# Two-layer decoder trunk on one core: gates of the first three expert groups kept on chip, first chunk's dots two steps later, scatter adds regrouped

## The chip, the core and the metric

The kernel runs on one core of a Trainium2 chip. A core has TensorE (PE: matmuls, with weight loads beside them), VectorE (DVE), ScalarE (ACT), GpSimd (POOL) and SyncE (SP); each runs its own queue of instructions in order, and they wait for each other by semaphores. SP, ACT and POOL also issue DMA transfers. The metric is the device time of one execution in microseconds (us), the median of several runs; less is better.

## The reference

512 tokens of width 1024 pass through two layers. Layer 0 mixes tokens with causal mean pooling and retention, layer 1 with a gated linear recurrence. After each mixer stands a PEER channel mixer, and after each of the four a layer norm. The change touches PEER alone:

```python
q = (xt @ w_q).reshape(T, PEER_HEADS, 2, PEER_HALF)
s = jnp.einsum('thpd,hpkd->thpk', q, sub_keys)
s_top, i_top = lax.top_k(s, PEER_TOPK)
...
best, pos = lax.top_k(cand, PEER_TOPK)
eid = jnp.take_along_axis(cand_id, pos, axis=-1)
gate = jax.nn.softmax(best, axis=-1)
...
act = jax.nn.gelu(jnp.einsum('td,thkd->thk', xt, u_sel), approximate=False)
coef = gate * act
return jnp.einsum('thk,thkd->td', coef, v_sel)
```

Each token has 8 heads. A head scores two sets of 128 sub-keys, takes the 16 best of each, and of their 256 sums the 16 best again: 16 of 16384 experts with a softmax gate. An expert is a row `u` and a row `v`; the output is the sum of gate x gelu(x.u) x v over the 128 chosen experts of a token.

## The kernel before

**Dense and gathered tokens.** For tokens 64 to 383 the kernel computes x.u for all 16384 experts, multiplies by a gate matrix that is zero where an expert wasn't chosen, and multiplies the product by all of `v`. For the last 128 tokens it fetches the chosen rows of `u` and `v` one by one. For the first 64 tokens it fetches the chosen `u` rows while it routes, and takes their `v` part in the dense product. Every fp32 operand of a matmul is split into a high and a low part (`split`, lines 172 to 174: `hi` on ACT, `lo` on VectorE), and each product is three matmuls (lines 189 to 191 in `mm3`, line 1142 in `mm2`).

**Groups and tiles.** Experts come in 128 blocks of 128, four blocks to a group (`NB`), so 32 groups (`NG`). `mm1` streams a block of `peer_ut`, multiplies and puts gelu(x.u) into `ge`. The gates of a group are a tile `gt` of 12 slices of 32 tokens by 4 blocks: slices 0 to 3 (the first 128 tokens) come from the DRAM array `gz`, slices 4 to 11 from the DRAM array `gd`.

**Routing** (`route_topk`). The query projection comes in four chunks of two heads. For each chunk, `steps` takes the 16 best for the token blocks 0, 1, 2, 3 (`top16`, four yields each), and `choose` picks the experts of the first block right after its own step. `Scatter.place` then fetches 16 rows of `u` per chunk on POOL (`urow`, line 745; two token halves share a row tile, and eight tiles go round), `Scatter.dots` multiplies them on VectorE (line 109), spread over later steps by the table `DOTS[chunk][token block][step]`. `Scatter.weigh` multiplies gelu into the gates (lines 115 and 117), and `Scatter.add` scatters gates into `gz` by accumulating indirect DMAs on POOL (line 131), 32 per chunk, 128 per layer, in portions after the table `ADDS`. Adds of one head don't wait for each other; the first of a head waits for those of the head before to have landed. Adds are queued behind the last row fetch (`issue_after(self.fetch)`).

**Dense gates** (`route_gates`). For each of eight slices VectorE builds one-hot matrices (`oh`, `og`, lines 924 and 925), TensorE multiplies them, ACT scales the result into the slice buffer `gbuf` (two buffers, line 936), and SP writes it to `gd` for all 32 groups (line 940).

**Lookahead.** While this runs, `lookahead` computes `mm1` for the first 25 groups (`NLA`). A generator yields costs, and for each 2.8 of credit one block of lookahead is issued: `Y2`, `YA` and `YB` are such costs. Groups 23 and 24 stay on chip (`KEEP`); the others are written to the DRAM array `sp` and read back. What is left is issued behind the routing.

**Experts** (`experts`). The groups come in a fixed order that begins with 28, 23, 24: group 28's blocks aren't looked ahead, so its `mm1` comes at the start of this stage, on TensorE in front of the first `mm2`. `fetch` reads a group's `ge` and `gt`: for the first two groups `gd` on SP and `gz` on POOL, for the others on ACT. `Scatter.read` (line 142) waits for all adds of the last head. `high` multiplies gates and `ge` on VectorE (line 1087) and casts the high part `ch` on ACT (line 1091), `low` makes `cl` on VectorE (line 1098), and `mm2` multiplies `ch`, `cl` by the two parts of `v` (line 1142). Between these, `gather_rounds` fetches the rows for the last 128 tokens on POOL (line 992) with dots (line 1004) and sums (line 1017) on VectorE.

The code is traced in the order in which it stands; a scheduler then places the instructions into the engines' queues by their dependences and priorities, so a queue's order may differ from the code's. Pools of tiles are opened and closed like a stack: the memory of a closed pool is used again, and the new user waits for the old one.

Of the kernel before, what the change touches and what calls it, by code (L numbers as in the profile page):

```python
# [9 lines left out]
F32 = mybir.dt.float32  # L10
F32R = mybir.dt.float32r
F16 = mybir.dt.float16
# [8 lines left out]
P = 128  # L21
# [8 lines left out]
NB = 4  # L30
# [9 lines left out]
NSD = TD // 32  # L40
NLA = 25
NSZ = 4
KEEP = 2
ROT = 3
RAW = 5
QS = 8
Y2 = 1.45
YA = 2.3
DOTS = (((0,) * 4, (0, 1, 2, 2), (3, 3, 3, 2), (0,) * 4), ((0,) * 4, (0,) * 4, (1,) * 4, (2,) * 4),
        ((1,) * 4, (0,) * 4, (1,) * 4, (2,) * 4), ((1,) * 4, (0,) * 4, (2,) * 4, (2,) * 4))  # L50
ADDS = ((0, 0, 16), (2, 14), (0, 17), (0, 128))
YB = (1.4, 1.4, 1.4, 4.0)
AHEAD = 6
TAIL = 4
# [92 lines left out]
class Kern:  # L147
# [547 lines left out]
    def peer(self, layer, xT, hs, out):  # L695
        nc, tc, io = self.nc, self.tc, self.io
        gd = self.dram.tile([NG, P, NSD - NSZ, NB, 32], F32, name="gd%d" % layer, tag="gd%d" % layer)
        sp = self.dram.tile([NLA, P, NB, TN], F32, name="sp%d" % layer, tag="sp%d" % layer)
        with tc.tile_pool(name="pe", bufs=1) as pe:
            self.pe = pe  # L700
            self.eid = pe.tile([P, P], I32, name="eid", tag="eid")
            self.gate3 = pe.tile([P, P], F32, name="gate3", tag="gate3")
            self.x3 = pe.tile([P, D], F32, name="x3", tag="x3")
            g, b = self.load_ln(layer, 0)

            def norm(tb):
                self.layernorm(tb, hs[tb], g, b, xT)
                if tb == NTB - 1:
                    nc.scalar.copy(self.x3, hs[tb])
                    nc.scalar.mul(hs[tb], hs[tb], ALPHA)  # L710

            self.out_proj(io["c_w_out" if layer else "ab_w_out"], xT, hs, norm)
            self.kept = {}
            self.urows = 0
            self.xx = pe.tile([P, D], F32, name="xx", tag="lng")
            for q in range(QN):
                nc.scalar.copy(self.xx[q * NU:(q + 1) * NU], hs[0][:NU])
            look = self.lookahead(layer, xT, sp)
            with tc.tile_pool(name="rk", bufs=1) as rk:
                gz = Scatter(self, rk, layer)  # L720
                kT = rk.tile([P, (TD - P) // GW, 4, GW], F16, name="kT", tag="kT")
                iot = rk.tile([P, P, 2], F16, name="iot", tag="iot")
                nc.gpsimd.iota(iot, pattern=[[1, P], [0, 2]], base=0, channel_multiplier=0,
                               allow_small_or_imprecise_dtypes=True)
                credit = CREDIT0
                for gen in (self.route_topk(layer, xT, kT, gz), self.route_gates(layer, kT, iot, gd)):
                    for cost in gen:
                        credit += cost
                        while credit >= 2.8:
                            credit -= 2.8  # L730
                            next(look, None)
            for _ in look:
                pass
            g1, b1 = self.load_ln(layer, 1)
            self.experts(layer, xT, hs, gd, gz, sp, lambda tb: self.layernorm(
                tb, hs[tb], g1, b1, None if layer else xT, out if layer else None))
        return xT

    def urow(self, pool, layer, ids, j):
# [31 lines left out]
    def route_topk(self, layer, xT, kT, gz):  # L771
        nc, tc, io = self.nc, self.tc, self.io
        with tc.tile_pool(name="rt", bufs=1) as rt, tc.tile_pool(name="rt2", bufs=2) as rt2, \
# [103 lines left out]
            def steps(c, tb, ps, cost, early=0):  # L877
                for i, top in enumerate(top16(c, tb, ps)):
                    if early == "w" and c < 3:
                        w0.append(self.stream(wq[c + 1, i]))  # L880
                    with tc.issue_after(top):
                        gz.dots(self, DOTS[c][tb][i])
                    yield cost

            for c in range(4):
                yield from steps(c, 0, scores(0), YA)
                if c > 1:
                    gz.weigh(self, rs2)
                gz.add(self, ADDS[c][0])
                yield from choose(0, c * 2, 2)  # L890
                gz.add(self, ADDS[c][1])
                yield from steps(c, 1, scores(1), YA, "w")
                late = [scores(tb) for tb in (2, 3)]
                if c < 3:
                    self.w0, w0 = w0, []
                    keys = project(c + 1)
                for tb in (2, 3):
                    yield from steps(c, tb, late[tb - 2], YB[c])
                    if c == 0 and tb == 2:
                        gz.weigh(self, rs2)  # L900
                        gz.add(self, ADDS[c][2])
            gz.weigh(self, rs2)
# [4 lines left out]
    def route_gates(self, layer, kT, iot, gd):  # L907
        nc, tc = self.nc, self.tc
        W, L = GW, 2
        Q = W // L  # L910
        with tc.tile_pool(name="rg", bufs=2) as rg:
            b5 = [P, 2, Q, P, L]
            for s in range(NSD - NSZ):
                gbuf = rg.tile([P, P, 32], F32, name="gbuf", tag="gbuf")
                for q in range(32 // W):
                    t0 = s * 32 + q * W

                    def per(i):
                        v = kT[:, t0 // W, i:i + 2, :].rearrange("p i (q l) -> p i q l", l=L)
                        return v[:, :, :, None, :].broadcast_to(b5)  # L920

                    oh = rg.tile([P, 2, Q, P, L], F16, name="oh", tag="oh")
                    og = rg.tile([P, 2, Q, P, L], F16, name="og", tag="og")
                    nc.vector.tensor_tensor(oh, iot[:, None, None].broadcast_to(b5), per(0), ALU.is_equal)
                    nc.vector.tensor_tensor(og, oh[:, 1:2].broadcast_to(b5), per(2), ALU.mult)
                    for r in range(W // 4):
                        if q % 2 and r == W // 4 - 1:
                            pg = self.psC.tile([P, 512], F32, name="pC", tag="pC")
                        else:
                            pg = self.psB.tile([P, 512], F32, name="pB", tag="pB")  # L930
                        for i in range(4):
                            a, b = divmod(r * 4 + i, L)
                            sl = slice(i * P, (i + 1) * P)
                            nc.tensor.matmul(pg[:, sl], oh[:, 0, a, :, b], og[:, 0, a, :, b], start=True, stop=False)  # L934
                            nc.tensor.matmul(pg[:, sl], oh[:, 0, a, :, b], og[:, 1, a, :, b], start=False, stop=True)
                        nc.scalar.mul(gbuf[:, :, q * W + r * 4:q * W + r * 4 + 4],
                                      pg.rearrange("p (t k) -> p k t", t=4), 1.0 / GS)
                    if q % 2:
                        yield 2 * Y2
                nc.sync.dma_start(out=gd[:, :, s].rearrange("g p b t -> p g b t"),  # L940
                                  in_=gbuf.rearrange("p (g b) t -> p g b t", b=NB))

    def lookup(self, pool, pos, i0, i1, thr, i16):
        nc = self.nc
# [75 lines left out]
    def experts(self, layer, xT, hs, gd, gz, sp, norm):  # L1020
        nc, tc, io = self.nc, self.tc, self.io
        with tc.tile_pool(name="ex", bufs=2) as ex, tc.tile_pool(name="ga", bufs=2) as ga:
            ex.tile([P, 48], F32, name="gap", tag="gap")
            accs = [[(self.psC if hf else self.psB).tile([P, 512], F32, name="pC" if hf else "pB",
                                                          tag="pC" if hf else "pB") for hf in range(2)]
                    for _ in range(3)]
# [14 lines left out]
            def fetch(n):  # L1041
                if n >= NG:
                    return
                g = order[n]
                if g in kept:
                    ge = self.kept[g]
                else:
                    ge = self.pe.tile([P, NB, TN], F32, name="ge", tag="ge", bufs=3)
                q = nc.scalar if n > 1 else nc.sync
                if g < NLA and g not in kept:  # L1050
                    q.dma_start(out=ge, in_=sp[g])
                gt = ex.tile([P, NSD, NB, 32], F32, name="gt", tag="gt", bufs=3)
                q.dma_start(out=gt[:, NSZ:], in_=gd[g])
                gz.read(q if n > 1 else nc.gpsimd, gt[:, :NSZ], g)
                ges[g] = (ge, gt)

            def cost(i):
# [47 lines left out]
            for i in range(NE):  # L1105
# [6 lines left out]
                g, b = order[i // NB], i % NB  # L1112
# [162 lines left out]
```

## Time and profile before

| what | value |
|---|---|
| median of 3 runs | 2740.01 us (2739.19 to 2741.67) |
| profiled execution, its own time | 2737.88 us |
| its span, first to last instruction | 2735.9 us |
| mean granted TensorE clock | 0.992 |
| layer 0: dense gates begin / first matmul of the expert stage | 563.74 / 683.98 us |
| layer 1: dense gates begin / first matmul of the expert stage | 1979.10 / 2098.87 us |
| DMA moved | 833.19 MB, mean 305 GB/s |

The profile is of one execution. A timeline row gives start and length of an instruction, its engine, the line of the kernel, what it writes and reads with the shapes, and in brackets how long the engine stood idle before it and what seems to have released it. SPq, ACTq and POOLq are the sequencers that issue DMAs. A row of waits gives the total, the number and the longest. Matmuls are pipelined: the length of one is longer than the distance to the next. A wait for several things at once is put down to the one that came last by the profile, which can be wrong where the named one had long been done.

### The profile page before, as it was taken

The numbers are of one execution on the slowest core, as the hardware profiler recorded it, in microseconds if no ns is written. First come the engines' busy times: TensorE is split into PE (matmuls) and PEld (weight loads), VectorE is DVE, ScalarE is ACT, GpSimd is POOL, SyncE is SP. The second block draws the span as 40 slices with busy tenths as digits, with TensorE's granted clock in tenths as the row PEclk, the third lists the DMA queues.
The fourth block names the chain that finished last, engine by engine and source line by source line (L and its number), as shares of the span: only waits on it lengthen the run. The fifth ranks groups of instructions, "written<-read, shape, count | busy, mean of one in ns | idle before, by whom it ended". The sixth has DMA issues, their size and how long they took to land.

```text
span 2735.9 us, 41888 instructions
## 1 busy us (share of the span) xinstructions
PE 2675.9 (98%) x15314; PEld 2376.5 (87%) x15314; DVE 2417.7 (88%) x4684; ACT 1091.4 (40%) x1539; POOL 1432.0 (52%) x929
## 2 busy tenths in 40 slices
PE   9999999999999999999999999999999999999998
PEld 7898999999888888787888889999998888888887
DVE  6678899997899999999798679999996899999999
ACT  3343444654333333333334344344554333333332
POOL 0006777786565666565000016777874566666553
PEclk9999999999999999999999999999999999999999
DMA  6357888799999999999322547889899999999995
GB/s 234 114 201 265 276 279 291 205 264 329 388 412 413 417 416 415 408 417 357 104 79 75 210 160 245 276 270 314 216 269 351 398 414 415 417 415 417 411 416 210
DMA packets 330991, 833.19 MB, mean 305 GB/s; under 512 B 63520, under 2 KB 129568, under 8 KB 330784
## 3 DMA queue, kind: packets, MB, share of 16 engines
q1 hardware_dynamic: 177536, 416.39, 42.9%
q0 software_dynamic: 129344, 336.78, 34.2%
q10 hardware_dynamic: 23904, 77.34, 7.1%
q8 instruction: 120, 1.97, 0.3%
q14 instruction: 87, 0.71, 0.1%
HBM read 747.69 MB, written 82.71 MB: 304 GB/s over the span
## 4 chain that ended last, share of the span: by engine, by line
PE 60%; DVE 12%; issue 11%; DMA 10%; POOL 5%; ACT 0%; DVEq 0%; POOLq 0%; SPq 0%; ACTq 0%
PE pB L1142 9%; PE pC L1142 9%; PE pA L191 9%; PE pA L189 9%; PE pA L190 9%; DMA row<-in_v,eid 7%; POOL row L992 5%; DVE lo L174 3%; PE pC L191 3%; PE pC L189 3%; PE pC L190 3%; DVE h L1017 2%; DMA urow<-in_u,ids 1%; DMA raw<-in_peer_v 1%; PE pB L934 1%
## 5 line engine op out<-in xcount | busy, mean ns | idle before, releaser
L173 ACT CAST hi<-raw 128x1024 fp32r<-128x1024 f32 (+1 forms) x609 | 636.4, 1051 | 959.8 <-PE pC L1142 137.2
L174 DVE TENSOR_TENSOR lo<-raw,hi 128x1024 fp32r<-128x1024 f32 (+1 forms) x609 | 728.7, 1214 | 92.8 <-ACT hi L173 88.6
L131 POOL DMA_INDIRECT gz<-gate,idx x256 | 505.4, 1974 | 155.0 <-issue 72.8
L992 POOL DMA_INDIRECT row<-in_v,eid x256 | 407.9, 1593 | 337.2 <-DVE av L1004 273.8
L191 PE MATMUL pA<-xThi,lo 128*128 128x320 f32 (+2 forms) x1680 | 550.7, 328 | 11.4 <-DVE lo L174 11.4
L189 PE MATMUL pA<-xThi,hi 128*128 128x320 f32 (+2 forms) x1680 | 551.7, 328 | 1.9 <-ACT hi L173 1.9
L190 PE MATMUL pA<-xTlo,hi 128*128 128x320 f32 (+2 forms) x1680 | 549.4, 327 | 0.0
L992 POOL DMA_INDIRECT row<-in_u,eid x256 | 350.4, 1369 | 136.3 <-issue 66.7
L1017 DVE SCALAR_TENSOR_TENSOR h<-row,cf,h 128x1024 f32<-128x1024 f32 x256 | 329.2, 1286 | 44.7 <-DMA row<-in_v,eid 38.5
L191 PEld LDWEIGHTS pA<-xThi,lo 128*128 128x128 f32 x1680 | 316.9, 189 | 28.2 <-DVE lo L174 13.8
L189 PEld LDWEIGHTS pA<-xThi,hi 128*128 128x128 f32 x1680 | 317.0, 189 | 18.0 <-ACT hi L173 2.8
L190 PEld LDWEIGHTS pA<-xTlo,hi 128*128 128x128 f32 x1680 | 316.9, 189 | 15.1
L1004 DVE CUSTOM_DVE_ANT_0 row<-row,x 128x1024 f32<-128x1024 f32 x256 | 310.7, 1217 | 13.1 <-DMA row<-in_u,eid 12.5
L1142 PE MATMUL pB<-lo,ch 128*128 128x512 f32 x768 | 302.0, 393 | 15.7 <-DVE lo L174 15.7
L1142 PE MATMUL pB<-hi,ch 128*128 128x512 f32 x768 | 301.3, 392 | 7.7 <-ACT ch L1091 7.7
L1142 PE MATMUL pB<-hi,cl 128*128 128x512 f32 x768 | 301.2, 392 | 0.0
L1142 PE MATMUL pC<-hi,cl 128*128 128x512 f32 x768 | 301.1, 392 | 0.0
L1142 PE MATMUL pC<-hi,ch 128*128 128x512 f32 x768 | 300.9, 392 | 0.0
L1142 PE MATMUL pC<-lo,ch 128*128 128x512 f32 x768 | 300.9, 392 | 0.0
L745 POOL DMA_INDIRECT urow<-in_u,ids x128 | 158.0, 1235 | 246.6 <-ACT ids L92 190.4
L191 PE MATMUL pC<-xThi,lo 128*128 128x320 f32 x800 | 249.7, 312 | 11.2 <-DVE lo L174 11.2
L189 PE MATMUL pC<-xThi,hi 128*128 128x320 f32 x800 | 250.2, 313 | 0.0
(280 smaller groups left out, 4603.1 us busy)
## 6 DMA issues: line engine op xcount, KB each, us to landing
raw<-in_peer_ut SPq DMA_DIRECT2D x256, 512.0 KB
raw<-in_peer_v SPq DMA_DIRECT2D x256, 512.0 KB
gd<-gbuf SPq DMA_DIRECT2D x16, 2048.0 KB
gt<-gd ACTq DMA_DIRECT2D x60, 512.0 KB
sp<-ge SPq DMA_DIRECT2D x46, 640.0 KB
ge<-sp ACTq DMA_DIRECT2D x46, 640.0 KB
raw<-in_peer_w_q SPq DMA_DIRECT2D x32, 512.0 KB
gz<-zero SPq DMA_DIRECT2D x64, 256.0 KB
```

The costliest lines, as they stand in the source:

```text
L131: d = nc.gpsimd.indirect_dma_start(out=flat, out_offset=bass.IndirectOffsetOnAxis(ap=self.idx[c][:, col], axis=0), in_=gate[:, col], in_of ...
L173: self.nc.scalar.copy(hi, src)
L174: return self.nc.vector.tensor_tensor(lo, src, hi.bitcast(F32), ALU.subtract)
L189: nc.tensor.matmul(ps, ah, bh, start=(first and i == 0), stop=False)
L190: nc.tensor.matmul(ps, ah, bl, start=False, stop=False)
L191: nc.tensor.matmul(ps, al, bh, start=False, stop=(last and i == n - 1))
L745: d = self.nc.gpsimd.indirect_dma_start(out=t, out_offset=None, in_=self.io["u%d" % layer], in_offset=bass.IndirectOffsetOnAxis(ap=ids[:, ...
L934: nc.tensor.matmul(pg[:, sl], oh[:, 0, a, :, b], og[:, 0, a, :, b], start=True, stop=False)
L992: nc.gpsimd.indirect_dma_start(out=t, out_offset=None, in_=io[name], in_offset=bass.IndirectOffsetOnAxis(ap=at, axis=0))
L1004: dot = nc.vector.tensor_tensor_reduce(ur, ur, x, 1.0, 0.0, ALU.mult, ALU.add, av[:, k:k + 1])
L1017: nc.vector.scalar_tensor_tensor(acc, vr, c, acc, ALU.mult, ALU.add)
L1142: nc.tensor.matmul(acc[hf], a[:, ts], b[:, hf * 512:(hf + 1) * 512], start=first and i == 0, stop=last and i == 2)
```

## The change

Before the dense gates are computed, three tiles `gt` are taken from a new pool `gx` for groups 28, 23 and 24, which are the first three of the expert stage. After each slice, ACT copies the parts of these groups from `gbuf` into them, beside the write to `gd`, which stays whole. In `fetch` these groups no longer read `gd`; their `gz` part is read on POOL, for the third group as well. The pool stays open through the expert stage, whose later groups take the same three buffers in turn; so does the routing's pool `rk`, which held `kT`, `iot` and the zeros. The one-hot tiles get a pool of their own ahead of the slice buffers', and the spacer `gap` of the expert stage has another size.

In chunk 0 the dots move from the second and third token blocks' steps to the third's and fourth's, and its `weigh` and first 16 adds from behind the third to behind the fourth. The adds go by whole heads: in chunk 1 two no longer go ahead of the row fetches and 14 behind them, but 16 behind; in chunk 2 it is 16, not 17. The cost `Y2` of the dense gates goes from 1.45 to 1.4.

```diff
-Y2 = 1.45
+Y2 = 1.4
-DOTS = (((0,) * 4, (0, 1, 2, 2), (3, 3, 3, 2), (0,) * 4), ((0,) * 4, (0,) * 4, (1,) * 4, (2,) * 4),
+DOTS = (((0,) * 4, (0,) * 4, (2, 2, 3, 3), (3, 3, 0, 0)), ((0,) * 4, (0,) * 4, (1,) * 4, (2,) * 4),
-ADDS = ((0, 0, 16), (2, 14), (0, 17), (0, 128))
+ADDS = ((0, 0, 16), (0, 16), (0, 16), (0, 128))
...
-            with tc.tile_pool(name="rk", bufs=1) as rk:
+            with tc.tile_pool(name="rk", bufs=1) as rk, ExitStack() as late:
...
+                def routing():
+                    yield from self.route_topk(layer, xT, kT, gz)
+                    self.gx = late.enter_context(tc.tile_pool(name="gx", bufs=1))
+                    self.first = {g: self.gx.tile([P, NSD, NB, 32], F32, name="gt", tag="gt", bufs=3)
+                                  for g in (NLA + ROT, NLA - 2, NLA - 1)}
+                    yield from self.route_gates(layer, kT, iot, gd)
...
-                    if c == 0 and tb == 2:
+                    if c == 0 and tb == 3:
                         gz.weigh(self, rs2)
                         gz.add(self, ADDS[c][2])
...
-        with tc.tile_pool(name="rg", bufs=2) as rg:
+        with tc.tile_pool(name="ro", bufs=2) as ro, tc.tile_pool(name="rg", bufs=2) as rg:
...
+                for g, gt in self.first.items():
+                    nc.scalar.copy(gt[:, NSZ + s], gbuf[:, g * NB:(g + 1) * NB, :])
...
-            ex.tile([P, 48], F32, name="gap", tag="gap")
+            ex.tile([P, 88], F32, name="gap", tag="gap", bufs=1)
...
-                gt = ex.tile([P, NSD, NB, 32], F32, name="gt", tag="gt", bufs=3)
-                q.dma_start(out=gt[:, NSZ:], in_=gd[g])
-                gz.read(q if n > 1 else nc.gpsimd, gt[:, :NSZ], g)
+                if g in self.first:
+                    gt = self.first[g]
+                    gz.read(nc.gpsimd, gt[:, :NSZ], g)
+                else:
+                    gt = self.gx.tile([P, NSD, NB, 32], F32, name="gt", tag="gt", bufs=3)
+                    q.dma_start(out=gt[:, NSZ:], in_=gd[g])
+                    gz.read(q, gt[:, :NSZ], g)
```

More of the change, by code (lines that the diff above doesn't have):

```diff
@@ L725, in peer @@
                 credit = CREDIT0
[L726 to L736, printed above, removed]
+                def routing():
[4 more added lines that the diff above has]
+                    yield from self.route_gates(layer, kT, iot, gd)
+                for cost in routing():
+                    credit += cost
+                    while credit >= 2.8:
+                        credit -= 2.8
+                        next(look, None)
+                for _ in look:
+                    pass
+                g1, b1 = self.load_ln(layer, 1)
+                self.experts(layer, xT, hs, gd, gz, sp, lambda tb: self.layernorm(
+                    tb, hs[tb], g1, b1, None if layer else xT, out if layer else None))
         return xT
@@ L920, in per @@
                         return v[:, :, :, None, :].broadcast_to(b5)
-                    oh = rg.tile([P, 2, Q, P, L], F16, name="oh", tag="oh")
-                    og = rg.tile([P, 2, Q, P, L], F16, name="og", tag="og")
+                    oh = ro.tile([P, 2, Q, P, L], F16, name="oh", tag="oh")
+                    og = ro.tile([P, 2, Q, P, L], F16, name="og", tag="og")
                     nc.vector.tensor_tensor(oh, iot[:, None, None].broadcast_to(b5), per(0), ALU.is_equal)
```

## The prediction

> **What bounds the kernel now.** I read the page first: span, engine shares, and who waited for whom on TensorE.
>
> ```profile
> span 2735.9 us, 41888 instructions
> PE 2675.9 (98%) x15314; PEld 2376.5 (87%) x15314; DVE 2417.7 (88%) x4684; ACT 1091.4 (40%) x1539; POOL 1432.0 (52%) x929
> ```
> ```profile
> PE pC L191 <- DVE lo L174: 11.2, 6, 4.7
> PE pB L1142 <- ACT ch L1091: 7.7, 2, 4.1
> ```
>
> TensorE is the bound: 98% busy, so all its idle time is 60 us and a change that leaves its work alone can win no more than that, plus slow matmuls after each gap. Two of its waits are long and occur once per layer: the matmul of line 191 behind the low half made on VectorE (up to 4.7), and the first matmul of the expert stage behind `ch` (up to 4.1). The change works on these two places, so I opened the timeline there, by engine.
>
> **The start of the expert stage.** Timeline of layer 0: start, length, engine, line, operation, and in brackets the idle time before it.
>
> ```profile
> 656.15 0.38 SPq L940 DMA_DIRECT2D gd<-gbuf  x1
> 658.91 1.55 POOL L131 DMA_INDIRECT gz<-gate,idx  x1 [0.30 <-issue]
> 668.07 0.62 POOL L142 DMA_DIRECT2D gt<-gz  x1 [7.61 <-DMA raw<-in_peer_v]
> 670.02 0.60 POOL L142 DMA_DIRECT2D gt<-gz  x1
> 666.92 1.23 DVE L174 TENSOR_TENSOR lo<-raw,hi 128x1024 fp32r<-128x1024 f32 x1 [2.29 <-ACT hi L173]
> 679.23 0.82 DVE L1087 TENSOR_TENSOR gt<-gt,ge 128x640 f32<-128x640 f32 x1 [11.09 <-DMA gt<-gz]
> 679.57 0.31 PE L191 MATMUL pA<-xThi,lo 128*128 128x320 f32 x1
> 683.98 0.80 PE L1142 MATMUL pB<-hi,ch 128*128 128x512 f32 x1 [4.10 <-ACT ch L1091]
> 687.01 0.40 PE L1142 MATMUL pC<-hi,ch 128*128 128x512 f32 x1
> 687.25 0.40 PE L1142 MATMUL pB<-lo,ch 128*128 128x512 f32 x1
> ```
>
> The last slice is sent to DRAM at 656.15, the last scatter add ends at 660.46, yet POOL stands for 7.61 until 668.07 before it asks for the first group's `gz` part; at that moment SP asks for the `gd` part too. The tile that both fill lies on the memory of the slices, so I read the 7.61 as the wait for the last slice to have left, not for the stream that the row names. VectorE has made its last low half at 666.92, waits 11.09 for the reads, and TensorE, done at 679.88, stands 4.10. Its next seven matmuls (683.98 to 687.01) take 3.03 against 7 x 0.24 at the pace of the last two rows: 1.35 more. The gap costs 5.45. Layer 1:
>
> ```profile
> 2066.75 1.95 POOL L131 DMA_INDIRECT gz<-gate,idx  x1 [0.30 <-issue]
> 2083.07 0.62 POOL L142 DMA_DIRECT2D gt<-gz  x1 [14.37 <-DMA raw<-in_peer_v]
> 2098.87 0.50 PE L1142 MATMUL pB<-hi,ch 128*128 128x512 f32 x1 [3.62 <-ACT ch L1091]
> 2103.36 0.41 PE L1142 MATMUL pB<-hi,ch 128*128 128x512 f32 x1
> ```
>
> Adds end at 2068.70, the read goes out 14.37 later; TensorE idles 3.62, and twelve matmuls take 4.49 instead of 2.88: 5.2 in all.
>
> **What the change does there.** Two things go: the read of `gd` for three groups, and the wait for the slices' memory, since the kept tiles lie elsewhere. What stays is the read of `gz`, which needs the last head's adds to have landed. Between two heads POOL shows what landing takes:
>
> ```profile
> 622.16 4.85 POOL L131 DMA_INDIRECT gz<-gate,idx  x1 [5.38 <-DMA gz<-gate,idx]
> ```
>
> So in layer 0 the first read can leave at 660.46 + 5.38 = 665.84, only 2.2 sooner. The second now follows it directly, 0.93 later (0.62 and the 0.30 of issue), without the row fetch between: 666.8 against 670.02, 3.2 sooner. The trace puts the first multiply behind the second read, and the first matmul 4.75 behind that multiply (679.23 to 683.98). Moved by 3.2, it starts at 680.8: 0.9 of idle left. The bytes that leave the queues may take that too:
>
> ```profile
> gt<-gd SPq DMA_DIRECT2D x4, 512.0 KB
> ```
>
> These are the first two groups' reads in both layers; in each layer two of 512 KB stood beside the `gz` reads. I take half of the 0.9: gain 5.0, between 2 (the reads keep their latency and the ramp stays) and 5.45. In layer 1 the read can leave at 2074.1, nine earlier; the gap of 5.2 goes whole. **Together 10.2.**
>
> The slow matmuls have a name: the Trainium skill, "TensorE: Matmul & The Clock Gate", Part 1, says that after an idle window of about 3.4 us the array runs at half rate until it has been busy that long. The trace agrees (3.03 for what takes 1.68). By that rule a leftover gap of 0.9 brings no slow matmuls, which is what the sum has.
>
> What it adds: 24 copies of 128 x 128 per layer on ACT. The nearest row:
>
> ```profile
> L842 ACT ACTIVATE gs<-pC 128x128 f32<-128x128 f32 x4 | 1.2, 292 | 0.0
> ```
>
> 24 x 0.292 = 7 us per layer on an engine that is 40% busy. They delay the PSUM evacuations and high halves queued behind them on ACT, three copies (0.9) at a time, and VectorE and TensorE wait for those. Between 0 and 14 for both layers, if all were in the way; I take 1, since ACT's share leaves room.
>
> Holding the tiles longer, the routing pool's tiles kept through the expert stage, and the new order of pools cost no instruction. Y2 moves at most one lookahead block from the gate loop to behind it; TensorE does the same work.
>
> **The first chunk's dots.** VectorE and TensorE of layer 0, then TensorE of layer 1:
>
> ```profile
> 217.95 1.23 DVE L109 CUSTOM_DVE_ANT_0 urow<-urow,xx 128x1024 f32<-128x1024 f32 x1 [2.77 <-DMA urow<-in_u,ids]
> 220.62 1.22 DVE L109 CUSTOM_DVE_ANT_0 urow<-urow,xx 128x1024 f32<-128x1024 f32 x1 [1.44 <-DMA urow<-in_u,ids]
> 223.24 0.64 PE L191 MATMUL pC<-xThi,lo 128*128 128x320 f32 x1 [4.15 <-DVE lo L174]
> 226.07 0.31 PE L189 MATMUL pC<-xThi,hi 128*128 128x320 f32 x1
> 226.22 0.31 PE L190 MATMUL pC<-xTlo,hi 128*128 128x320 f32 x1
> ...
> 1638.40 0.63 PE L191 MATMUL pC<-xThi,lo 128*128 128x320 f32 x1 [4.70 <-DVE lo L174]
> 1642.73 0.31 PE L189 MATMUL pC<-xThi,hi 128*128 128x320 f32 x1
> ```
>
> Two dots wait for fetched rows (2.77 and 1.44), the low half behind them is late, TensorE idles 4.15 and runs ten matmuls in 2.83 instead of 1.5: 5.5. Layer 1: 4.70, and sixteen in 4.33 instead of 2.4: 6.6. With the dots two steps on, both gaps go. But something is late next:
>
> ```profile
> 249.89 1.62 POOL L131 DMA_INDIRECT gz<-gate,idx  x1 [12.50 <-DVE stop L871]
> 260.15 0.18 DVE L873 CAST itop<-ix 128x64 f16<-128x64 uint32 x1
> 281.13 1.55 POOL L131 DMA_INDIRECT gz<-gate,idx  x1 [0.30 <-issue]
> 285.03 1.54 POOL L131 DMA_INDIRECT gz<-gate,idx  x1 [2.35 <-DMA gz<-gate,idx]
> 288.73 1.02 POOL L745 DMA_INDIRECT urow<-in_u,ids  x1 [0.30 <-issue]
> 296.61 1.21 DVE L109 CUSTOM_DVE_ANT_0 urow<-urow,xx 128x1024 f32<-128x1024 f32 x1
> 307.64 1.23 DVE L109 CUSTOM_DVE_ANT_0 urow<-urow,xx 128x1024 f32<-128x1024 f32 x1 [0.19 <-DMA urow<-in_u,ids]
> ...
> 1695.29 1.65 POOL L131 DMA_INDIRECT gz<-gate,idx  x1 [0.30 <-issue]
> 1704.28 1.47 POOL L745 DMA_INDIRECT urow<-in_u,ids  x1 [0.30 <-issue]
> ```
>
> The weighing, and with it the first 16 adds, moves from behind the third step (249.89) to behind the fourth. That step ends at 260.33; all 16 dots lie ahead of it either way, so it moves earlier only by the vanished waits, about 4.2: 256, and the first add to about 257, 7 later. On POOL's queue these adds stand ahead of the next chunk's 16 row fetches. Taking two adds away wins back 288.73 - 282.68 = 6.05. So chunk 1's fetches start at about 290, one later than now, while TensorE comes 5.5 sooner. Chunk 1's sixth dot (307.64) already waits 0.19 for its row: no slack. VectorE should wait there for about what it saved before, with the same kind of low halves behind it. Layer 1: 1704.28 - 1696.94 = 7.3 won, 7 lost. Ends: -1.5 and +5.5 in layer 0, 0 and +6.6 in layer 1. **I take 0 for both**, nearest to the row without slack.
>
> **The 17th add.** In chunk 2 one add of the next head goes:
>
> ```profile
> 424.90 1.57 POOL L131 DMA_INDIRECT gz<-gate,idx  x1 [6.22 <-DVE iy L103]
> 452.86 0.42 PE L191 MATMUL pA<-xThi,lo 128*128 128x320 f32 x1 [1.00 <-DVE lo L174]
> ```
>
> It waited 6.22 for the head before it to land and held chunk 3's fetches by 1.9; TensorE then has small gaps, this one 1.00. Worth 0 to 1.9 per layer; I take 1.0. The add returns behind those fetches, so the last add ends where it did. **Together 2.**
>
> **What the expert stage keeps.** Granted clock and DMA by stretch (last columns: clock, DMA share, GB/s):
>
> ```profile
> 900.00:1300.00 400.00, 388.52 (x1818) 329.54 (x1817) 377.04 (x438) 135.73 (x162) 243.34 (x164) 0.98 1.01 404
> ```
>
> DMA is full here, and TensorE idles 11.5. If TensorE begins 5 sooner but its rows don't, it waits here instead. DMA loses 3 x 512 KB per layer, 3.9 us at 404 GB/s, and rows start a little sooner; at most 1.5 per layer is missing. I take half, 1.5 in all.
>
> **Sum.** 10.2 + 0 + 2 - 1 - 1.5 = 9.7 less than the profiled execution's 2737.88 (span 2735.9): 2728.2. The median shown, 2740.01, lies 2.1 above it: **2730**.
>
> **Rivals.**
> - *The dots' gap is won whole*: chunk 1's rows come in time, or the low halves are queued ahead of the dots. For it: two adds and their landing wait are gone. Against it: the 0.19. 12.1 more: 2718.
> - *The stage takes it back*: DMA sets the end of the expert stage, and the 10.2 return as waits for rows. For it: 404 GB/s, 1.01. Against it: fewer bytes. 2740 - 2 + 1 = 2739. The Trainium skill, "DMA: Bandwidth & Descriptors", section "Issuing engines are not separate DMA queues", says that all queues run on the same 16 engines; by that, only the bytes removed count, not the queue that they leave.
> - *Slower: the multiply comes too early in VectorE's order*. It no longer depends on slices read back, and the trace shows that VectorE's order is not the code's: at 679.23 the later group's multiply stands ahead of two low halves. Set ahead of the last blocks' low halves, it would stop VectorE until about 676 in layer 0. A block is 24 matmuls of 0.15, 3.6. With two behind it TensorE runs dry at 672.7 and gets its next low half at about 678 (multiply 0.82, low half 1.23): a gap about as long as now, the point from which it decides. With four: dry at 665.5, 12.5 idle instead of 4.1, and in layer 1, by the same steps, some 6.4 instead of 3.6. 11 lost, 2 won, 1 paid: 2750. Against it: now every low half stands ahead.
> - *The reads leave no sooner*, because the adds end later or the 7.61 was their landing: only layer 1's 14.37 has room then. 5 lost: 2735.
>
> **Chances.** Forecast 0.5 (2723 to 2737 by the copies' and the dots' ends), gap won whole 0.2, taken back 0.12, reads no sooner 0.1, slower 0.08. A measurement of this kernel tells about 0.2%, 5.5 us, from no change. Faster: 0.45 of the forecast's 0.5, the 0.2, and 0.05 of the fourth: 0.7. Slower 0.09. Same 0.21. Range 2717 to 2740: it leaves out the slow rival and a little below.
>
> **What would show it.** Right: the first matmul of line 1142 in each layer with under 1 us idle before it; POOL's reads some 5 us after its last add; no wait of line 109 near 218 but one near 292 with TensorE idle behind it, near 311; no add between chunk 2's sixteen and chunk 3's fetches. Wrong: TensorE without that second gap (then 2718), idle time grown between 900 and 1300, or low halves of line 174 behind a waiting line 1087's multiply.

## The result, and the profile after

The changed kernel takes **2725.03 us** (median of 6 runs, 2722.67 to 2731.21) where the kernel before, measured beside it, takes 2741.36 (6 runs, 2739.19 to 2744.15). The ratio is 0.9943, 95% interval 0.993 to 0.9957: about 16 us faster. The forecast was 2730, the range 2717 to 2740. The profiled execution took 2723.48 against 2737.88. Its page and its waits of TensorE (total, times, longest):

```profile
span 2721.7 us, 41924 instructions
PE 2669.3 (98%) x15314; PEld 2370.1 (87%) x15314; DVE 2417.0 (89%) x4684; ACT 1101.9 (40%) x1587; POOL 1451.0 (53%) x931
...
DMA packets 330000, 830.05 MB, mean 305 GB/s; under 512 B 63424, under 2 KB 129472, under 8 KB 329792
```
```profile
PE pB L1155 <- DVE lo L174: 19.7, 10, 4.5
PE pA L191 <- DVE lo L174: 12.3, 11, 3.5
PE pC L191 <- DVE lo L174: 5.1, 5, 1.9
```

The two long waits of before are gone: no wait for `ch` is left, and the wait of `pC` in line 191 has a longest of 1.9 where it had 4.7. What has grown is `pB` behind low halves, in the expert stage; in the kernel before it was

```profile
PE pB L1142 <- DVE lo L174: 15.7, 7, 4.5
```

Where the 14.2 us of the span went is read from the same instructions in both timelines (start of the instruction, us from the start of the span). During chunk 0's steps TensorE already computes chunk 1's projection, and so on:

| point on TensorE | layer 0 before | after | layer 1 before | after |
|---|---|---|---|---|
| end of chunk 1's projection, in chunk 0's steps | 248.49 | 243.09 | 1664.28 | 1651.01 |
| end of chunk 2's, in chunk 1's steps | 316.07 | 313.74 | 1731.87 | 1721.80 |
| end of chunk 3's, in chunk 2's steps | 384.27 | 384.31 | 1800.06 | 1790.94 |
| last lookahead matmul | 665.64 | 663.04 | 2081.00 | 2070.36 |
| first matmul of the expert stage | 683.98 | 677.12 | 2098.87 | 2084.43 |
| last one | 1312.81 | 1306.47 | 2726.58 | 2711.36 |

Layer 0 wins 5.4 in chunk 0's steps and has lost all of it by the end of chunk 2's; it wins 2.6 between there and the end of the lookahead, and 4.3 more at the start of the expert stage. Layer 1 starts 6.3 ahead, wins 6.9 in chunk 0, keeps 2.8 of them, wins 1.5 and then 3.8.

The start of the expert stage in layer 0, timeline of the changed kernel, POOL, VectorE and TensorE:

```profile
651.04 1.98 POOL L131 DMA_INDIRECT gz<-gate,idx  x1 [0.30 <-issue]
658.71 1.75 POOL L142 DMA_DIRECT2D gt<-gz  x3 [5.68 <-DMA raw<-in_peer_v]
666.86 1.59 POOL L1001 DMA_INDIRECT row<-in_u,eid  x1 [6.40 <-issue]
...
665.59 0.82 DVE L1100 TENSOR_TENSOR gt<-gt,ge 128x640 f32<-128x640 f32 x1 [11.73 <-DMA gt<-gz]
666.33 4.62 DVE L174 TENSOR_TENSOR lo<-raw,hi 128x1024 fp32r<-128x1024 f32 x4
671.22 1.23 DVE L174 TENSOR_TENSOR lo<-raw,hi 128x1024 fp32r<-128x1024 f32 x1 [0.27 <-ACT hi L173]
...
676.98 0.31 PE L191 MATMUL pA<-xThi,lo 128*128 128x320 f32 x1
677.12 0.39 PE L1155 MATMUL pB<-hi,ch 128*128 128x512 f32 x1
```

The three reads follow the last add by 5.68, as forecast, but that add ends at 653.02, not at 660.46. VectorE's multiply stands *ahead* of five low halves, the order that the slower rival feared. TensorE passes from lookahead to expert stage without idling, and its first matmul takes 0.39.

The first chunks and chunk 3, same kernel:

```profile
255.11 2.35 POOL L131 DMA_INDIRECT gz<-gate,idx  x1 [14.05 <-DVE gate L117]
292.94 1.00 POOL L752 DMA_INDIRECT urow<-in_u,ids  x1 [0.30 <-issue]
301.47 1.23 DVE L109 CUSTOM_DVE_ANT_0 urow<-urow,xx 128x1024 f32<-128x1024 f32 x1 [7.10 <-DMA urow<-in_u,ids]
...
282.43 0.41 PE L191 MATMUL pA<-xThi,lo 128*128 128x320 f32 x1 [1.24 <-DVE lo L174]
287.07 0.41 PE L191 MATMUL pC<-xThi,lo 128*128 128x320 f32 x1 [0.86 <-DVE lo L174]
360.56 0.42 PE L191 MATMUL pC<-xThi,lo 128*128 128x320 f32 x1 [1.88 <-DVE lo L174]
...
419.03 1.54 POOL L131 DMA_INDIRECT gz<-gate,idx  x1 [0.30 <-issue]
424.76 1.00 POOL L752 DMA_INDIRECT urow<-in_u,ids  x1 [4.19 <-ACT ids L92]
```

Adds and fetches start 5 and 4 later than before, VectorE waits 7.10 for the first row, and TensorE's 4.15 has come back as pieces of 0.2 to 1.9 in chunks 1 and 2 (4.7 in all). Those at 282.43 and 287.07 come before VectorE's first wait for a row, and VectorE has no idle time between 268 and 290: there its own work is late, not a row. In chunk 3 no add stands between the sixteen and the fetches; POOL waits 4.19 there all the same, for `ids`, the numbers of the rows.

### The profile page after: what moved, and what is told of

It reads as the page before. It is cut to its first block, busy times and chain, and to the rows that moved or that the text cites. A ratio compares the mean times of both kernels' runs of the same rounds, so it can differ in the third digit from the quotient of the medians.

```text
span 2721.7 us, 41924 instructions
## 1 busy us (share of the span) xinstructions
PE 2669.3 (98%) x15314; PEld 2370.1 (87%) x15314; DVE 2417.0 (89%) x4684; ACT 1101.9 (40%) x1587; POOL 1451.0 (53%) x931
## 4 chain that ended last, share of the span: by engine, by line
PE 44%; DVE 19%; issue 15%; DMA 13%; POOL 8%; ACT 1%; DVEq 0%; POOLq 0%; SPq 0%; ACTq 0%
DMA row<-in_v,eid 10%; PE pA L191 8%; PE pA L189 8%; PE pA L190 8%; POOL row L1001 8%; DVE lo L174 5%; PE pB L1155 4%; PE pC L1155 4%; DVE h L1026 3%; PE pC L191 3%; PE pC L189 3%; PE pC L190 3%; DMA urow<-in_u,ids 2%; DVE urow L109 2%; DVE row L1013 2%
## 5 line engine op out<-in xcount | busy, mean ns | idle before, releaser
L131 POOL DMA_INDIRECT gz<-gate,idx x256 | 514.0, 2008 | 139.3 <-issue 88.8
```

Source lines behind the costliest of these rows:

```text
L131: d = nc.gpsimd.indirect_dma_start(out=flat, out_offset=bass.IndirectOffsetOnAxis(ap=self.idx[c][:, col], axis=0), in_=gate[:, col], in_of ...
```

## The experiments

Each kernel was timed in five rounds beside the kernel before on the same chip; ratios are to that, with 95% intervals. "Later" and "sooner" compare profiled executions. All kernels are compared by ratio, so small differences between the sets of runs (medians of the kernel before: 2739.97 to 2742.11) drop out; the changed kernel itself was not timed again in them. A ratio's interval is about 3.5 us to either side. One set has e1 (new dots and adds alone), e2 (kept tiles alone), e3 (old adds) and e4 (denser dots); a second, on another chip, e5 (the read), e6 (more bytes), e7 (copies twice) and e9 (the 17th add); a third, on the chip of the first, e8 (old constants), e10 (swapped pools) and e11 (both denser dots and swapped pools); the fourth, on a third chip, e12 (e11 with tiles moved).

**The two halves, each alone.** First the kernel before with the new dots and adds only:

```diff
-DOTS = (((0,) * 4, (0, 1, 2, 2), (3, 3, 3, 2), (0,) * 4), ((0,) * 4, (0,) * 4, (1,) * 4, (2,) * 4),
+DOTS = (((0,) * 4, (0,) * 4, (2, 2, 3, 3), (3, 3, 0, 0)), ((0,) * 4, (0,) * 4, (1,) * 4, (2,) * 4),
-ADDS = ((0, 0, 16), (2, 14), (0, 17), (0, 128))
+ADDS = ((0, 0, 16), (0, 16), (0, 16), (0, 128))
...
-                    if c == 0 and tb == 2:
+                    if c == 0 and tb == 3:
```

> The kernel before with the dots, the weighing and the adds of the change alone; gates as before. Theory 1 (the dots' gap is won in chunk 0 but given back in chunks 1 and 2, because chunk 1's row fetches stand on POOL behind sixteen adds that begin later; the add moved out of chunk 2 is worth about 2 us per layer): 4 to 7 us faster than the kernel before, about 2735 us where the kernel before takes 2741, and the gaps of 4.1 and 3.6 us at the start of the expert stage still there. Rival (the dots' gap is won for good, 5.5 and 6.6 us): 12 us faster or more, about 2729 us.

2733.78 us, ratio 0.9974 (0.9963 to 0.9984): 7 won. Then the changed kernel with the old dots, adds and `Y2` (the lines above turned round, and `Y2 = 1.45`), so that only the kept tiles are left:

> The changed kernel with the dots, adds and Y2 of the kernel before: the kept gates alone. Theory 1 (the gaps at the start of the expert stage, 5.5 and 5.2 us with their slow matmuls, go, and the stage gives back under 2 us each): 7 to 10 us faster than the kernel before, about 2733 us; the gaps of 4.1 and 4.7 us behind the fetched rows of chunk 0 are there again. Rival (the stage is set by DMA and takes the gaps back as waits for rows): 0 to 3 us faster, about 2739 us.

2733.45, ratio 0.9967 (0.9954 to 0.998): 9 won. 7 + 9 is the whole gain; the halves add up. The starts of the expert stage, both layers of the first, then layer 0 of the second:

```profile
683.09 0.80 PE L1142 MATMUL pB<-hi,ch 128*128 128x512 f32 x1 [4.67 <-ACT ch L1091]
2092.84 0.80 PE L1142 MATMUL pB<-hi,ch 128*128 128x512 f32 x1 [3.53 <-ACT ch L1091]
```
```profile
681.96 0.39 PE L1155 MATMUL pB<-hi,ch 128*128 128x512 f32 x1
```

Without the kept tiles both gaps stay, with the slow matmuls behind them (0.80); with them both go, whatever the adds do. In the first kernel the last add ends at 654.15, 6.3 sooner than before, yet the read leaves only at 667.18, 13 later:

```profile
667.18 0.62 POOL L142 DMA_DIRECT2D gt<-gz  x1 [13.03 <-DMA raw<-in_peer_v]
```

There the wait for the slices' memory shows by itself, with the adds long landed: the last slice was sent at 654.69, and the read follows it by 12.5, as in the kernel before by 11.9.

**The adds.** The changed kernel with the old `ADDS`:

```diff
-ADDS = ((0, 0, 16), (0, 16), (0, 16), (0, 128))
+ADDS = ((0, 0, 16), (2, 14), (0, 17), (0, 128))
```

> The changed kernel with the old table of adds, so that two adds stand ahead of chunk 1's row fetches and one ahead of chunk 3's; the dots stay two steps on. Theory 1 (chunk 1's fetches have no slack, and the one add ahead of chunk 3's fetches costs 1.5 to 2.6 us per layer): 5 to 10 us slower than the changed kernel, about 2732 us where that takes 2725. Rival (VectorE itself is full there, and POOL's order decides nothing): within 2 us of the changed kernel.

2736.66, ratio 0.9983 (0.9974 to 0.9993): 11 slower than the changed kernel, a little more than expected. Timeline of layer 0:

```profile
299.52 1.54 POOL L131 DMA_INDIRECT gz<-gate,idx  x1 [6.23 <-DMA gz<-gate,idx]
303.21 1.00 POOL L752 DMA_INDIRECT urow<-in_u,ids  x1 [0.30 <-issue]
...
326.29 0.63 PE L191 MATMUL pA<-xThi,lo 128*128 128x320 f32 x1 [4.18 <-DVE lo L174]
```

The next head's first add waits 6.23 for the head before to land; the fetches start 10 later and TensorE stands 4.18. So dots two steps on need whole heads: with the old adds they give the gap back at once. Only the 17th add of chunk 2 put back:

```diff
-ADDS = ((0, 0, 16), (0, 16), (0, 16), (0, 128))
+ADDS = ((0, 0, 16), (0, 16), (0, 17), (0, 128))
```

> The changed kernel with one add of the next head again ahead of chunk 3's row fetches, and nothing else. Theory 1 (it waits for the sixteen before it to land and holds the fetches, for which VectorE waits): 2 to 5 us slower than the changed kernel, with TensorE's gaps between 450 and 465 us back. Rival (the whole loss of the old table came from the two adds in chunk 1): within 1.5 us.

2730.87, ratio 0.9963 (0.995 to 0.9976): 5.5 slower than the changed kernel by the ratios, where the forecast had 2; the two intervals overlap a little.

```profile
426.43 1.54 POOL L131 DMA_INDIRECT gz<-gate,idx  x1 [6.30 <-DVE iy L103]
428.27 1.82 POOL L752 DMA_INDIRECT urow<-in_u,ids  x1 [0.30 <-ACT ge L765]
...
663.35 1.75 POOL L142 DMA_DIRECT2D gt<-gz  x3 [5.93 <-DMA raw<-in_peer_v]
```

The fetches start at 428.27 instead of 424.76; 1.4 of this was lost before the add (chunk 3's projection ends at 385.72 instead of 384.31), and some 2 are the add's. From the end of that projection to the first matmul of the expert stage it takes 3.0 and 2.6 longer than in the changed kernel, 5.6 for both layers, which is what the ratios say. The last add ends at 657.43 instead of 653.02 and the reads leave 4.6 later. In layer 1 they leave 15.8 later, but that layer starts 6.9 later; the profiled execution, 2735.58, was the slowest of the five. From chunk 3's last fetch to the end of the routing POOL issues adds alone, so a microsecond lost ahead of them isn't made up there by other work.

**The dots, denser.** All sixteen dots of chunk 0 on the third step, four a block, and `weigh` back behind that step, so that its adds start sooner:

```diff
-DOTS = (((0,) * 4, (0,) * 4, (2, 2, 3, 3), (3, 3, 0, 0)), ((0,) * 4, (0,) * 4, (1,) * 4, (2,) * 4),
+DOTS = (((0,) * 4, (0,) * 4, (4,) * 4, (0,) * 4), ((0,) * 4, (0,) * 4, (1,) * 4, (2,) * 4),
...
-                    if c == 0 and tb == 3:
+                    if c == 0 and tb == 2:
```

> The changed kernel with chunk 0's sixteen dots all in the third token block's steps, four each, and the weighing and the first sixteen adds behind that block again. Theory 1 (late fetches of chunk 1 take the gain back): the first add begins at about 246 us instead of 255, chunk 1's fetches at about 284 instead of 293, and 3 to 5 us per layer stay, about 2718 us where the changed kernel takes 2725. Rival (VectorE's load in chunks 0 and 1 takes it back): the same as the changed kernel within 2 us, with TensorE's small gaps before 292 us unchanged, or slower because four dots a step wait for rows.

2722.84, ratio 0.9924 (0.9911 to 0.9937): some 5 faster than the changed kernel by the ratios, though the intervals overlap a little.

```profile
251.37 1.62 POOL L131 DMA_INDIRECT gz<-gate,idx  x1 [10.29 <-DVE stop L875]
285.14 1.48 POOL L752 DMA_INDIRECT urow<-in_u,ids  x1 [0.30 <-issue]
...
288.12 0.42 PE L191 MATMUL pC<-xThi,lo 128*128 128x320 f32 x1 [0.85 <-DVE lo L174]
```

Fetches start 8 sooner than in the changed kernel, and no dot waits 7 us for its row. But in layer 0 TensorE ends chunk 3's projection at 383.22 (384.31), only 1.1 sooner, and in layer 1 it keeps 2.8 of what it won, as in the changed kernel. In chunk 2's steps its idle time falls from 2.45 to 0.57; in chunk 1's it stays (2.29 and 2.60), though VectorE now idles 2.7 there instead of 10.3. So the late fetches, which the prediction named, were less than half of what the moved dots cost in layer 0. The rest is VectorE's own work, as the rival said. Where the 5 come from the two profiled executions don't show: they took 2724.34 and 2723.48.

**The read and the copies.** The changed kernel with the kept tiles but the `gd` read in place of the copies:

```diff
-                for g, gt in self.first.items():
-                    nc.scalar.copy(gt[:, NSZ + s], gbuf[:, g * NB:(g + 1) * NB, :])
...
                     gt = self.first[g]
+                    q.dma_start(out=gt[:, NSZ:], in_=gd[g])
```

> The changed kernel without the copies on ScalarE: the three kept tiles stay in their own pool, but their gates are read back from DRAM as before. Theory 1 (both parts matter: the wait for the slices' memory held the reads of gz, and the read of gd itself lands about 8 us after the last slice is written): a gap of 2 to 4 us at the start of the expert stage comes back in each layer, 3 to 8 us slower than the changed kernel. Rival (the memory alone mattered, and the copies only move bytes): within 1.5 us of the changed kernel.

2730.9, ratio 0.9969 (0.9958 to 0.9979): 7 slower. Its two starts:

```profile
680.08 0.49 PE L1154 MATMUL pB<-hi,ch 128*128 128x512 f32 x1 [2.01 <-ACT ch L1103]
2089.80 0.49 PE L1154 MATMUL pB<-hi,ch 128*128 128x512 f32 x1 [2.39 <-ACT ch L1103]
```

The kernel before idles 4.10 and 3.62 there. So the wait for the memory was about half of the gap in layer 0 and a third in layer 1, and the read is the rest. The time doesn't split alike, because slow matmuls come behind these shorter gaps too. Two stretches of this run, with the granted clock third from the end:

```profile
681.16:684.57 3.41, 3.41 (x9) 2.70 (x9) 3.10 (x3) 1.53 (x4) 0.00 (x0) 0.50 1.02 417
2090.87:2094.28 3.41, 3.41 (x9) 2.73 (x9) 3.10 (x3) 1.53 (x4) 0.00 (x0) 0.50 1.03 419
```

And the copies made twice (48 a layer):

> The changed kernel with each copy of a slice's gates made twice, 48 copies per layer instead of 24. Theory 1 (ScalarE has room, the copies hide): within 1.5 us of the changed kernel. Rival (a burst of copies delays what is queued behind it, with about 6 us of ScalarE per layer in the way): 3 us slower or more.

2723.86, ratio 0.9944 (0.9931 to 0.9957): the same. The groups of ACT, first of the changed kernel, then of this one (both layers; total us, mean ns, idle before):

```profile
L950 ACT COPY gt<-gbuf 128x128 f32<-128x128 f32 x48 | 11.3, 306 | 0.5
```
```profile
L951 ACT COPY gt<-gbuf 128x128 f32<-128x128 f32 x96 | 20.9, 304 | 0.5
```

9.6 us more of ACT's time, and no cost that the interval shows.

**More bytes.** The forecast let the expert stage give back what DMA can't carry sooner. To test it, three transfers of 512 KB a layer, DRAM to DRAM, are written in the code where the changed kernel dropped the `gd` reads:

```diff
                     gt = self.first[g]
+                    more = self.dram.tile([P, 1024], F32, name="more%d%d" % (layer, g), tag="more%d%d" % (layer, g))
+                    q.dma_start(out=more, in_=io["peer_v"][layer, g])
```

> The changed kernel with three more transfers of 512 KB per layer, from DRAM to DRAM, issued where the removed reads of gd stood and waiting for nothing. Theory 1 (DMA shares the bound of the expert stage, so bytes early in it come back as waits for rows): 3 to 8 us slower than the changed kernel. Rival (the stage's waits come from the latency of single rows, and bytes don't matter): within 2 us.

2724.23, ratio 0.9943 (0.993 to 0.9956): equal to the changed kernel.

```profile
DMA packets 330192, 833.20 MB, mean 306 GB/s; under 512 B 63520, under 2 KB 129568, under 8 KB 329888
```

All 3.1 MB are there, but not in the expert stage. They wait for nothing, and the scheduler put all six at the start of the execution (ACT's queue, then SP's):

```profile
0.75 1.25 ACTq L1064 DMA_DIRECT2D more<-in_peer_v  x2
36.73 1.41 SPq L1064 DMA_DIRECT2D more<-in_peer_v  x2
56.65 1.68 SPq L1064 DMA_DIRECT2D more<-in_peer_v  x2
```

So this run tests neither of its two theories, and whether bytes bound the expert stage stays open. For the forecast's reason, rows that don't come sooner, speak VectorE's waits for fetched rows in layer 0's stage (700 to 1300 us), first of the kernel before, then of the changed one:

```profile
DVE h L1017 <- DMA row<-in_v,eid: 21.8, 15, 2.7
DVE row L1004 <- DMA row<-in_u,eid: 4.3, 5, 1.2
```
```profile
DVE h L1026 <- DMA row<-in_v,eid: 24.2, 17, 2.9
DVE row L1013 <- DMA row<-in_u,eid: 7.4, 7, 2.0
```

They grow from 26.1 to 31.6.

**What gives back in the expert stage.** POOL's first row fetch waits 6.40 (666.86), although the reads are out: the row tiles lie on the last slice's memory. In the next two kernels the two pools are opened the other way round, which moves the rows' memory and no instruction, first alone and then together with the denser dots:

```diff
-        with tc.tile_pool(name="ex", bufs=2) as ex, tc.tile_pool(name="ga", bufs=2) as ga:
+        with tc.tile_pool(name="ga", bufs=2) as ga, tc.tile_pool(name="ex", bufs=2) as ex:
```

> Only the order in which two pools are opened differs from the changed kernel, so every engine's queue is the same and the row tiles of the expert stage no longer lie on the memory of the last slice buffer. Theory (the stage gives back because the first rows wait for that memory, 6.4 us idle on POOL ahead of the fetch at 666.86): the first row fetch goes out near 661 us, TensorE's waits between 700 and 1320 us fall from 13.8 us towards the 11.4 us of before, and the time is 1.5 to 4 us under the changed kernel. Rival (the give-back is in how the stage runs, whenever its rows come): the fetch goes out earlier but the waits stay within 1 us of 13.8 and the time within 1.5 us of the changed kernel's.

> The earlier dots of the dense variant and the swapped pools together. If both act and add up: 2718 to 2721 us on a chip where the changed kernel takes 2725. Rival (the swap does nothing): as the dense variant alone, 2721 to 2724 us.

2731.28, ratio 0.9964 (0.9953 to 0.9976), and 2729.19, 0.9957 (0.9944 to 0.997): both *slower* than the same kernel without the swap, by about 6 and 9 (the first pair's intervals overlap a little). Neither theory had that. Fetches of the two:

```profile
667.03 1.75 POOL L142 DMA_DIRECT2D gt<-gz  x3 [6.87 <-DMA gz<-gate,idx]
669.09 1.03 POOL L1001 DMA_INDIRECT row<-in_u,eid  x1 [0.30 <-issue]
```
```profile
668.11 2.08 POOL L1001 DMA_INDIRECT row<-in_u,eid  x1 [9.58 <-PE pA L191]
```

No fetch left near 661. In the first the adds themselves ended late; in the second the rows wait for TensorE, by the releaser named in the row; in the built program they lie on the one-hot tiles, which its last routing matmuls read. So the runs don't test my theory of the give-back. In the same set of runs went the changed kernel with the two old constants:

```diff
-Y2 = 1.4
+Y2 = 1.45
...
-            ex.tile([P, 88], F32, name="gap", tag="gap", bufs=1)
+            ex.tile([P, 48], F32, name="gap", tag="gap")
```

> The changed kernel with the two planner constants of before (1.45 and 48). Both theories on record say that these two constants move no instruction: within 1 us of the changed kernel. If it is slower by 2 us or more, the constants act by where tiles lie in memory.

2732.48, ratio 0.9968 (0.9956 to 0.998): 7 slower, with the same instructions in the same order on every engine; the two intervals just touch. The filler tile `gap` decides where the tiles behind it start. In the built programs the rows start at an odd multiple of 32 bytes in e8, e10 and e11, and at a multiple of 64 in the kernel before, the changed kernel and all others. So the last run was e11 with the rows moved by 32 bytes, again with the same instructions (other tiles of the stage, `ch` among them, move too):

```diff
-            ex.tile([P, 88], F32, name="gap", tag="gap", bufs=1)
+            ga.tile([P, 8], F32, name="gap", tag="gap", bufs=1)
```

> The same instructions in the same order as the run with earlier dots and swapped pools (e11); only the filler tile is moved and shrunk, so that the seven row tiles start at a multiple of 64 bytes in a partition (178432 in place of 178400), as they do in the kernel before, in the changed kernel and in all runs that were not slowed in the expert stage. Theory (the rows' place slows the expert stage: 0.233 us between successive 128x512 matmuls of line 1155 in e8, e10 and e11 where the changed kernel has 0.227): the pitch is 0.227 again and the time 2719 to 2724 us where the kernel before takes 2741 (ratio 0.992 to 0.9935). Rival (that chip was slower in those minutes, or the pools' order costs): pitch 0.233, ratio 0.9950 to 0.9965. Side question: with the pitch back, if the swapped order lets the first rows go out early, under 2720; if not, as the dense variant (2722 to 2724).

**2717.59**, ratio 0.9918 (0.9904 to 0.9932), the fastest kernel here: 11 faster than e11, the intervals well apart, and within the interval of the dense variant without the swap. Its first fetch and its matmuls of line 1155 between 700 and 1300 us (total, mean ns, idle), beside those of the changed kernel and of e8:

```profile
666.21 2.06 POOL L1001 DMA_INDIRECT row<-in_u,eid  x1 [7.60 <-PE pA L191]
```
```profile
L1155 PE MATMUL pC<-hi,ch 128*128 128x512 f32 x363 | 144.3, 398 | 0.0
```
```profile
L1155 PE MATMUL pC<-hi,ch 128*128 128x512 f32 x363 | 142.1, 392 | 0.0
```
```profile
L1155 PE MATMUL pC<-hi,ch 128*128 128x512 f32 x361 | 143.4, 397 | 0.0
```

The time came as the theory said, but its reason did not. Successive 128x512 matmuls start 0.233 apart in e12 too, as in e8, e10 and e11, and 0.227 apart in the changed kernel. The stage is not longer for it: 628.1 and 626.0 from first to last matmul in e12, 629.4 and 626.9 in the changed kernel, because the waits shrink (3.8 and 3.4 us in e12, 12.8 and 14.3 there). What slowed e8, e10 and e11 is therefore not settled. From e11 to e12, 2 us went ahead of the stage and some 3 in each stage. Part of the first is idle time of TensorE for which the profile shows no cause, long before a row tile is used; e8 near 437 us:

```profile
436.39 0.30 PE L189 MATMUL pC<-xThi,hi 128*128 128x320 f32 x1 [0.70 <-issue]
437.82 0.31 PE L191 MATMUL pC<-xThi,lo 128*128 128x320 f32 x1 [0.97 <-issue]
```

e8, e10 and e11 have 2.4 to 3.1 us of it in all, no other kernel has any, and these three ran in one set. The kernel before ran at its usual 2742.11 in that set. Between e11 and e12 nothing but the place of tiles was changed in the kernel, but e12 ran later and on another chip, where the kernel before took 2740.16. So neither the place of the tiles nor the set of runs is ruled out as the cause.

## Why the prediction was right or wrong

- **Sign and size.** Faster, as forecast; 16 instead of 10. The result lies between the forecast and the rival that wins the dots' gap whole, but that rival isn't why. In the traces, 14.2 where 9.7 was said, the difference is 2.8 of the dots in layer 1, 2.1 of the 17th add, 1.0 of the copies and 0.9 at the start of the expert stage, less 1.2 that this stage kept and 1.0 at the end.
- **Start of the expert stage: right in its mechanism, a little low.** 10.2 was said. Measured: the first matmul wins 4.3 and 3.8 on the last lookahead matmul, and the slow matmuls of 1.35 and 1.6 go as well: 11.05. Memory and read are separate causes (the run with the read). By the Trainium skill, "TensorE: Matmul & The Clock Gate", Part 1, the array falls to half rate after an idle window of about 3.4 us. The traces show that shorter gaps do it too: 2.01 and 2.39 in the run with the read, each followed by 3.41 at a granted clock of 0.50. So the prediction's "a leftover gap of 0.9 brings no slow matmuls" has no threshold of 3.4 behind it, and no such gap was left to test it.
- **"The reads could leave at 665.84, only 2.2 sooner": wrong.** They left at 658.71, because the last add ended at 653.02, 7.4 sooner. The step that failed is "the add returns behind those fetches, so the last add ends where it did". What the forecast counted came as written: chunk 3's fetches start 2.0 sooner (424.76, 426.78) and not 6.22, because POOL now waits 4.19 for `ids` where it waited for the landing. The other 5 lie in the adds. From the end of chunk 3's fetches to the last add's end, 79 adds took 206.8 before and 80 take 201.9 after; in the ten kernels with the new adds this stretch takes 199.7 to 210.3, in the four with the 17th add 199.7 to 206.8. So the 5 are luck as far as the runs show. In layer 1 the last add ended 8.4 sooner, but that layer also starts 6.3 sooner. The stage didn't need it: in e10 the reads left at 667.03, and TensorE passed into the stage without idling as well.
- **The 17th add: 2 said, about 4 to 5.5 found.** 2.6 and 1.5 between chunk 2 and the lookahead's end in the table; put back alone, 5.5. The place was right and the term too small: in layer 0 TensorE's idle time behind low halves in that stretch is 2.73 before, 0.63 after, and 3.13 with the add put back.
- **First chunk's dots: 0 said, right in layer 0, low in layer 1, and in good part for another reason.** The chain came nearly as written: first add 255.11 (257 said), fetches 292.94 (290 said), VectorE waiting for rows, 5.4 won and 5.4 lost by chunk 2. But TensorE lost it in small pieces, not in one gap near 311, and 2.29 of the 4.7 idle before VectorE first waits for a row. The forecast had only the rows; the dense variant, whose rows come in time, still idles 2.60 there. In layer 1, 2.8 of 6.9 stayed.
- **Copies: 1 said, none seen**, even when doubled. That fits ACT's share of 40%, which alone doesn't prove it.
- **What the stage keeps: 1.5 said, about 2.7 found.** The stage is 0.5 longer and 0.8 shorter, though it begins without 1.35 and 1.6 of slow matmuls. VectorE waits 5.5 longer for rows in layer 0, which fits the forecast's reason. Whether DMA's bytes make the rows late wasn't tested, and what sets the stage's length of 626 to 633 us in every kernel stays open.
- **The slower rival: its order came, its gap didn't.** The multiply stood ahead of five low halves, but until 665.59 and not 676, because the adds ended sooner. In e8 it stood until 672.38, and TensorE idled 0.08 there: it had lookahead blocks enough.
- **"The new order of pools costs no instruction": true, and not the whole.** Kernels with the same instructions and tiles in other places differ by 7 (e8) to 11 us (e11 to e12), about half of the change or more, though the set of runs differs in both pairs. The prediction gave the filler tile no price and no place in the range.

The terms as measured: 11.05 + 2.8 + 4.1 - 2.7, less 1.0 between the last expert matmul and the end (9.3 before, 10.3 after), make the 14.2 of the span.

## What to carry to other kernels

A chained write (add after add to the same array) costs its landing wait only where the work queued behind it is ready: two adds ahead of chunk 1's fetches held them by 6 before and by 10 in e3, one ahead of chunk 3's by 2, because those would have waited for `ids` anyway. A wait that names a stream may be one for memory: move the tile, and see whether the wait goes. And when a change moves tiles, run the same instructions with the tiles elsewhere before giving the credit to the instructions. Extra work that is to load one stage must wait for something in that stage; look in the trace where it went.

## What the runs showed of the hardware

- The granted clock fell to 0.50 for 3.41 us or twice that behind gaps of TensorE of 4.10 and 4.67 us, but also behind 2.01 and 2.39 (e5) and 1.88 (e1, at 360.34). Behind 2.67 in the kernel before, at 2432.3, it stayed at 1.00.
- The expert stage's 128x512 matmuls start 0.227 us apart in ten kernels and 0.233 in e8, e10, e11 and e12; the 128x320 ones keep 0.147 in all. In the built programs of the ten, `ch` starts at a multiple of 512 bytes in a partition, in the four it doesn't. No run changed that alone.
- Most of POOL's scatter adds take 1.5 to 2.7 us (248 of 256 in the changed kernel), but one right behind a landing wait can take 5 to 6.4: 6.42 and 5.06 in e8, 6.00 and 5.42 in the dense variant; in the changed kernel 2.38 and 1.81 at the same two places. Its eight longer ones, 3.2 to 5.0, stand behind no wait. The dense variant was fast all the same.
